# Weight sums on VectorE, a turn inside an early tile, and row sums in two exact parts: one change to an encoder layer

## The chip, the cores and the metric

The kernel runs on one core of a Trainium2 chip. The core has five engines that run side by side: TensorE (PE: matrix products into the accumulators of PSUM; its weight loads, PEld, overlap the products), VectorE (DVE), ScalarE (ACT), GpSimd (POOL) and SyncE (SP, which here only issues transfers from memory). The metric is the device time of one execution in microseconds. Three runs of the kernel before gave 828.65, 829.03 and 829.23, median 829.03.

## The reference

One layer of a bidirectional encoder, 512 positions, width 1024, all in float32:

```
h  = rmsnorm(x, g_pre_mix)
q, k, v, g, u, sv, a_ret, a_sgu = split(h @ w_in)
y_ret = (layernorm(retention(q, k, v)) * silu(g)) @ w_ret_o      # both directions
sv    = layernorm(gelu(sv))                                      # with gain and bias
mixed = einsum('gpq,bnqgc->bnpgc', w_spatial, sv) + b_spatial
y_sgu = (gelu(u) * mixed) @ w_sgu_o
x1 = x  + rmsnorm((sig(a_ret)*y_ret + sig(a_sgu)*y_sgu) @ w_out, g_post_mix)
h2 = rmsnorm(x1, g_pre_ffn)
a, b = split(conv3(h2 @ w_up) + conv_b)
y  = x1 + rmsnorm((gelu(a) * b) @ w_down, g_post_ffn)
```

The mixing multiplies 128 x 128 weights per group with the normed sv. The bias of that norm is the same for all positions, so it enters the mixed result as bias times the row sum of the weights; these row sums are what the kernel calls `rws`.

## The kernel before

**Two parts for each number.** The kernel splits each operand into a high part in the format fp32r (a rounding copy on ScalarE) and a low part, the rest (a subtraction on VectorE): `split`, lines 84 to 86. A product is then three fp32r matmuls (high x high, high x low, low x high), `mm3`, lines 212 to 215. Two products are left in plain float32: the mixing itself (L736) and the row sums of its weights, a matrix of ones times the transposed weights `wst` (L713).

**Seven products for eight.** For u, the two gates and the 16 middle tiles of the up projection (in eight couples), a pair of weight blocks is multiplied in the Winograd way: a 2 x 2 arrangement of weight quarters B11, B12, B21, B22 takes seven products, with the sums of weights T1 = B11 + B12, T3 = B12 + B22, T2 = T1 + B22 and T4 = T2 + B21 (signs are in the stored weights). `w_form`, lines 153 to 171, loads a pair as two transfers of 128 x 1024, makes the sums (T1 and T3 on VectorE, lines 164 and 165; T2 and T4 on GpSimd, lines 166 and 168), and splits each form into a weight slot. `Pair`, lines 647 to 706, makes the products (L663). There are 20 pairs: four of u, eight of the gates, eight of the up projection.

**The order.** `units` lists all weight blocks and forms in the order in which PE needs them; `w_get` prepares them ahead, up to nine slots deep. Each weight form takes one of nine slots (tag `w4`), each raw block one of four raw buffers; a transfer from SP waits until its raw buffer is free. Within these limits the compiler's planner sets the order of each engine's instructions: each engine takes the next instruction in the program's order that by the planner's own times is ready, and on the chip each engine then runs its list strictly in that order, waiting on semaphores. So an instruction can overtake another in the list, but never on the chip.

**Where the change acts.** (1) `w_form`. (2) The row sums: L709 loads `wst`, L713 multiplies, L715 copies the result out. The program places them just ahead of u's pairs and behind the second `g_evac`, which multiplies o by the gate on VectorE (L609), turns it by 16 transposes on PE (L599) and splits it. (3) The start of the up projection. `norms` (lines 842 to 868) ends the mixing for 128 positions and norms them (xn); `turn` (lines 872 to 894) transposes these by eight matmuls (L879), copies the high part with ScalarE (L881), takes the low part with VectorE (L884), and makes a second copy for the Winograd sums (L892). While the last turns are under way, PE works on the first four tiles of the up projection, `early` (lines 898 to 907): first the columns of positions 0 to 255, which need turns 0 and 1, and later those of 256 to 511.

Lines 917 to 923 order that:

```
917    early(0, 0)
918    turn(2, zs[2])
919    for e in range(1, EARLY):
920        early(e, 0)
921    turn(3, zs[3])
922    for e in range(EARLY):
923        early(e, 1)
```

Of the kernel before, what the change touches and what calls it, by code (L numbers as in the profile page):

```python
# [11 lines left out]
F32R = mybir.dt.float32r  # L12
AF = mybir.ActivationFunctionType
ALU = mybir.AluOpType

P = 128
D = 1024
S = 512
NT = S // P
KD = D // P  # L20
# [17 lines left out]
EARLY = 4  # L38
# [9 lines left out]
def tile_block(ctx: ExitStack, tc, xT, x, wall, par, cs, wsp, bsp, gpost, gffn, out):  # L48
    nc = tc.nc
    sb = ctx.enter_context(tc.tile_pool(name="sb", bufs=1))  # L50
# [9 lines left out]
    def blk(dt=F32, n="blk", shape=(P, S)):  # L60
        return sb.tile(list(shape), dt, tag="blk", bufs=NBLK, name=nm(n))

    def tmp(n="tmp", shape=(P, S)):
        return sb.tile(list(shape), F32, tag="tmp", bufs=6, name=nm(n))

    def halves(n):
        return [blk(n=n), blk(n=n)]
# [4 lines left out]
    def ps(shape=(P, S)):  # L72
        return pp.tile(list(shape), F32, tag="ps", name=nm("ps"))

    def const(n, shape):
        return sb.tile(list(shape), F32, tag=n, bufs=1, name=n)
# [4 lines left out]
    def as32(t):  # L81
        return t.bitcast(F32)

    def split(hi, lo, src):
        copy(hi, src)
        nc.vector.tensor_sub(lo, src, as32(hi))  # L86
# [31 lines left out]
    w_ready, w_pos, w_held, w_raw = {}, [0, 0], [0], {}  # L118

    def raw_tile():  # L120
        return sb.tile([P, 1024], F32, tag="raw", bufs=4, name=nm("raw"))

    def slot(n, at=0, w=1024):
        return sb.tile([P, 1088], F32R, tag="w4", bufs=9, name=nm(n))[:, at : at + w]
# [28 lines left out]
    def w_form(form, i):  # L153

        if form == "B11":
            a, b = raw_tile(), raw_tile()
            nc.sync.dma_start(a, wall[i])
            nc.sync.dma_start(b, wall[i + 1])
            w_raw["B11"], w_raw["B12"] = a[:, :S], a[:, S:]
            w_raw["B22"], w_raw["B21"] = b[:, :S], b[:, S:]  # L160
        elif form == "T1":
            t = raw_tile()
            w_raw["T1"], w_raw["T2"], w_raw["T3"], w_raw["T4"] = t[:, :S], t[:, S:], w_raw["B12"], t[:, S:]
            nc.vector.tensor_add(w_raw["T1"], w_raw["B11"], w_raw["B12"])  # L164
            nc.vector.tensor_add(w_raw["T3"], w_raw["B12"], w_raw["B22"])
            nc.gpsimd.tensor_tensor(out=w_raw["T2"], in0=w_raw["T1"], in1=w_raw["B22"], op=ALU.add)  # L166
        elif form == "T4":
            nc.gpsimd.tensor_tensor(out=w_raw["T4"], in0=w_raw["T2"], in1=w_raw["B21"], op=ALU.add)
        w = slot("wf", 16)
        split(w[:, :S], w[:, S:], w_raw[form])  # L170
        return w[:, :S], w[:, S:]
# [21 lines left out]
    def w_unit(u):  # L193
        return w_block(u[1]) if u[0] == "blk" else (w_down if u[0] in "qt" else w_form)(*u)
# [4 lines left out]
    def w_get(look=LOOK):  # L199

        i = w_pos[0]
        w_pos[0] += 1
        room = 2 * look + (2 if w_size(units[i]) == 2 else 0)
        n = sum(w_size(u) for u in units[i : w_pos[1]])
        while w_pos[1] < len(units) and (w_pos[1] <= i or n + w_size(units[w_pos[1]]) <= max(room, 9 if look == LOOK else 0)):
            u = units[w_pos[1]]
            w_ready[w_pos[1]] = w_unit(u)
            w_pos[1] += 1
            n += w_size(u)
        return w_ready.pop(i)  # L210

    def mm3(o, ah, al, bh, bl, start, stop):
        nc.tensor.matmul(o, ah, bh, start=start, stop=False)  # L213
        nc.tensor.matmul(o, ah, bl, start=False, stop=False)  # L214
        nc.tensor.matmul(o, al, bh, start=False, stop=stop)  # L215
# [14 lines left out]
    def col(i):  # L230
        return part[:, i : i + 1]
# [30 lines left out]
    for k in range(KD):  # L262
# [18 lines left out]
        for m in range(8):  # L281
            c = slice(m * P, (m + 1) * P)
# [5 lines left out]
    T0, T1 = slice(0, 256), slice(256, 512)  # L288
# [15 lines left out]

    ident = const("ident", [P, P])
    make_identity(nc, ident)
    ones = const("ones", [P, P])
    nc.gpsimd.memset(ones, 1.0)
    wst = blk(n="wst")
    nhalf = const("nhalf", [P, 16])  # L310
    nc.gpsimd.memset(nhalf, -0.5)
# [10 lines left out]
    for t in range(NT):  # L322
        for n in range(2):
# [3 lines left out]
                out=xt, in_=xt, func=AF.Square, accum_out=ss[:, 4 * n + t : 4 * n + t + 1]  # L327
# [19 lines left out]
    for c in range(19, 1, -2):  # L347
        v.scalar_tensor_tensor(
            out=lc, in0=lc, scalar=1.0 / c, in1=lb, op0=ALU.add, op1=ALU.mult
# [4 lines left out]
        out=lg, in0=lc, scalar=-2.0, in1=lg, op0=ALU.mult, op1=ALU.add  # L354
# [5 lines left out]
    for m in range(8):  # L360
        t = blk(n="qkraw")
# [8 lines left out]
    for t in range(NT):  # L370
# [4 lines left out]
            start=True,  # L375
            stop=True,
# [249 lines left out]
    for n, acc in enumerate(t_group()):  # L626
        if n < 2:
            for k in (n + 2, n + 6):
                t = tmp("xT")
# [80 lines left out]
    bst = blk(n="bst")  # L710
    nc.gpsimd.dma_start(bst, bsp.rearrange("g p -> (g p)")[None, :].to_broadcast([P, S]))
    rw = ps()
    nc.tensor.matmul(rw, ones, wst, start=True, stop=True)  # L713
    rws = blk(n="rws")
    copy(rws, rw)  # L715
    uT, late = [], None
    for j in range(KD // 2):
        p = Pair(AF.Gelu_apprx_tanh, lambda: blk(n="u"), None, rbc)
# [51 lines left out]
    for j in range(KD // 2):  # L770
        for o, t in gated_pair(ogh, ogl, late if j == 0 else None):
            b = blk(n="r")
# [99 lines left out]
    def turn(t, zs):  # L872
        c = slice(t * P, (t + 1) * P)
        pf = []
        for n in range(2):
            p = ps()
            for f in range(4):
                pf.append(p[:, f * P : (f + 1) * P])
                nc.tensor.transpose(pf[-1], zs[n][:, f * P : (f + 1) * P], ident)  # L879
            for k in range(4 * n, 4 * n + 4):  # L880
                nc.scalar.activation(  # L881
                    out=h2h[k][:, c], in_=pf[k], func=AF.Copy, scale=col(FFNG + k)
                )
                v.scalar_tensor_tensor(  # L884
                    out=h2l[k][:, c], in0=pf[k], scalar=col(FFNG + k), in1=as32(h2h[k][:, c]),
                    op0=ALU.mult, op1=ALU.subtract,
                )
        for k in range(KD):
            if t == 0 and k % 2 == 0:
                h2.append(halves("h2"))  # L890
            at = (k % 2) * 256 + (t % 2) * P
            nc.scalar.activation(  # L892
                out=h2[k // 2][t // 2][:, at : at + P], in_=pf[k], func=AF.Copy, scale=col(FFNG + k)
            )

    early_w, early_o = [], []

    def early(e, q):

        if q == 0:  # L900
            early_w.append(w_get(1))
            early_o.append(ps())
        wh, wl = early_w[e]
        f = slice(q * 256, (q + 1) * 256)
        for k in range(KD):
            c = slice(k * P, (k + 1) * P)
            mm3(early_o[e][:, f], wh[:, c], wl[:, c], h2h[k][:, f], h2l[k][:, f], k == 0, k == KD - 1)

# [2 lines left out]
    for t in range(NT):  # L911
# [3 lines left out]
        acc.append(dn_.finish(t, 1))  # L915
        zs[t] = norms(t, acc)
    early(0, 0)
    turn(2, zs[2])
    for e in range(1, EARLY):
        early(e, 0)  # L920
    turn(3, zs[3])
    for e in range(EARLY):
        early(e, 1)

# [70 lines left out]
    while i < NF:  # L995
        if i in couples:
            p = Pair(None, lambda: tmp("c"), (h2h, h2l, h2forms))
# [179 lines left out]
def _parts(a, n, w):  # L1177

    k = a.shape[0] // P
    return a.reshape(k, P, n, w).transpose(2, 1, 0, 3).reshape(n, P, k * w)  # L1180
# [15 lines left out]
def _two(a):  # L1196

    b = _parts(a, 8, P).reshape(4, 2, P, 2, S)
    return np.stack([
        np.concatenate([b[:, 0, :, 0], b[:, 1, :, 0]], -1), np.concatenate([b[:, 1, :, 1], b[:, 0, :, 1]], -1),  # L1200
    ], 1)


def _up(a):

    for i, _ in COUPLES:
        b, c = a[2 * i].reshape(P, 2, S), a[2 * i + 1].reshape(P, 2, S)
        a[2 * i : 2 * i + 2] = np.stack([
            np.concatenate([b[:, 0], c[:, 0]], -1), np.concatenate([c[:, 1], b[:, 1]], -1),
        ])  # L1210
    return a


def _gates(a, w):

    return np.concatenate([_two(a), _parts(w, 8, P).reshape(4, 2, P, 1024)], 1).reshape(16, P, 1024)
# [79 lines left out]
```

## Time and profile before

| | |
|---|---|
| median of 3 runs | 829.03 us |
| profiled execution: its time, and its span from first to last instruction | 830.36 us, 828.6 us |
| PE busy | 818.5 us (99% of the span), 5152 matmuls |
| VectorE busy | 658.0 us (79%), 1100 instructions |
| ScalarE busy | 439.7 us (53%), 769 instructions |
| GpSimd busy | 101.1 us (12%), 102 instructions |
| the two GpSimd sums (L166, L168) | 36.5 and 26.5 us, 20 times each |
| PE's clock as granted | 0.998 |

A row of a timeline has the start in the span, the duration, engine, line, operation, what it writes and reads (by the program's names, buffer numbers left out), and in brackets how long the engine had been idle and what ended that. Several alike in a run stand in one row with their number. Matmuls are pipelined: one of 512 columns is shown as 0.39 us long, but the next starts 0.23 us later, so that it is the distance of the starts that counts. The same holds on VectorE in a smaller measure. A group's row ends with count, busy time and mean length in ns, and then the idle time ahead of its instructions and what ended it.

### The profile page before, as it was taken

The numbers are of one execution on the slowest core, as the hardware profiler recorded it, in microseconds if no ns is written. First come the engines' busy times: TensorE is split into PE (matmuls) and PEld (weight loads), VectorE is DVE, ScalarE is ACT, GpSimd is POOL, SyncE is SP. The second block draws the span as 40 slices with busy tenths as digits, with TensorE's granted clock in tenths as the row PEclk, the third lists the DMA queues.
The fourth block names the chain that finished last, engine by engine and source line by source line (L and its number), as shares of the span: only waits on it lengthen the run. The fifth ranks groups of instructions, "written<-read, shape, count | busy, mean of one in ns | idle before, by whom it ended". The sixth has DMA issues, their size and how long they took to land.

```text
span 828.6 us, 13261 instructions
## 1 busy us (share of the span) xinstructions
PE 818.5 (99%) x5152; PEld 737.4 (89%) x5152; DVE 658.0 (79%) x1100; ACT 439.7 (53%) x769; POOL 101.1 (12%) x102
## 2 busy tenths in 40 slices
PE   9999999999999999999999999999999999999996
PEld 7888888888899999999988898899999998999996
DVE  7479897877798777767766569979899889987967
ACT  6635445546665444444445585555556666555531
POOL 0010000102121111132210211120201200000001
PEclk9999999999999999999999999999999999999999
DMA  8733222212233332233349112333333341233344
GB/s 292 246 115 102 77 77 76 77 51 93 75 101 129 102 102 82 97 101 101 100 160 339 53 45 72 102 103 102 102 102 102 102 153 51 75 115 104 116 153 153
DMA packets 29215, 93.24 MB, mean 113 GB/s; under 512 B 3360, under 2 KB 4000, under 8 KB 29152
## 3 DMA queue, kind: packets, MB, share of 16 engines
q1 hardware_dynamic: 26928, 86.85, 31.6%
q0 software_dynamic: 1360, 4.46, 1.6%
q10 hardware_dynamic: 864, 1.09, 0.4%
q8 instruction: 40, 0.66, 0.3%
q14 instruction: 23, 0.19, 0.1%
HBM read 88.19 MB, written 4.19 MB: 112 GB/s over the span
## 4 chain that ended last, share of the span: by engine, by line
PE 92%; DVE 5%; ACT 1%; issue 1%; DMA 0%; POOL 0%; DVEq 0%; SPq 0%; POOLq 0%; ACTq 0%
PE ps L663 24%; PE ps L213 12%; PE ps L214 12%; PE ps L215 12%; PE ps L1033 8%; PE ps L475 5%; PE ps L474 5%; PE ps L476 5%; PE ps L1049 2%; PE ps L812 2%; PE ps L811 2%; PE ps L813 2%; PE ps L736 1%; DVE fl L86 1%; PE ps L275 1%; DVE dl L86 1%
## 5 line engine op out<-in xcount | busy, mean ns | idle before, releaser
L86 DVE TENSOR_TENSOR wl<-raw,wh 128x1024 fp32r<-128x1024 f32 (+1 forms) x93 | 108.0, 1170 | 53.1 <-PE ps L663 29.1
L79 ACT ACTIVATE wf<-raw 128x512 fp32r<-128x512 f32 x140 | 85.0, 627 | 98.8 <-PE ps L214 41.1
L86 DVE TENSOR_TENSOR wf<-raw,wf 128x512 fp32r<-128x512 f32 x140 | 109.0, 793 | 25.5 <-ACT wf L79 23.7
L663 PE MATMUL ps<-sh,wf 128*128 128x256 f32 x640 | 122.4, 281 | 0.0
L79 ACT ACTIVATE wh<-raw 128x1024 fp32r<-128x1024 f32 (+2 forms) x95 | 93.3, 991 | 38.7 <-DMA raw<-wall 19.1
L663 PEld LDWEIGHTS ps<-sh,wf 128*128 128x128 f32 x640 | 101.7, 188 | 0.8 <-ACT u L79 0.2
L213 PE MATMUL ps<-h2h,wh 128*128 128x512 f32 (+1 forms) x256 | 92.5, 364 | 0.4 <-ACT h2h L881 0.4
L214 PE MATMUL ps<-h2l,wh 128*128 128x512 f32 (+1 forms) x256 | 92.5, 363 | 0.0
L215 PE MATMUL ps<-h2h,wl 128*128 128x512 f32 (+1 forms) x256 | 92.3, 361 | 0.0
L663 PE MATMUL ps<-sl,wf 128*128 128x256 f32 x320 | 89.9, 281 | 0.0
L474 PE MATMUL ps<-wh,xh 128*128 128x512 f32 x192 | 75.0, 391 | 0.0
L475 PE MATMUL ps<-wl,xh 128*128 128x512 f32 x192 | 74.9, 390 | 0.0
L476 PE MATMUL ps<-wh,xl 128*128 128x512 f32 x192 | 74.8, 390 | 0.0
L166 POOL TENSOR_TENSOR raw<-raw,raw 128x512 f32<-128x512 f32 x20 | 36.5, 1825 | 237.5 <-DVE raw L164 209.3
L663 PEld LDWEIGHTS ps<-sl,wf 128*128 128x128 f32 x320 | 61.3, 192 | 0.6
L1033 PE MATMUL ps<-dl,fh 128*128 128x256 f32 x216 | 60.0, 278 | 0.1
L1033 PE MATMUL ps<-dh,fh 128*128 128x256 f32 x216 | 60.0, 278 | 0.0
L1033 PE MATMUL ps<-dh,fl 128*128 128x256 f32 x216 | 59.9, 277 | 0.0
L663 PE MATMUL ps<-xh,wf 128*128 128x256 f32 x288 | 55.3, 282 | 0.0
L215 PEld LDWEIGHTS ps<-h2h,wl 128*128 128x128 f32 x256 | 48.1, 188 | 7.7
L213 PEld LDWEIGHTS ps<-h2h,wh 128*128 128x128 f32 x256 | 47.8, 188 | 7.6 <-ACT h2h L881 0.7
L214 PEld LDWEIGHTS ps<-h2l,wh 128*128 128x128 f32 x256 | 48.1, 188 | 6.6
(307 smaller groups left out, 2048.2 us busy)
## 6 DMA issues: line engine op xcount, KB each, us to landing
raw<-wall SPq DMA_DIRECT2D x145, 512.0 KB, 3.6
x<-x SPq DMA_DIRECT2D x24, 256.0 KB, 5.4
xT<-xT SPq DMA_DIRECT2D x8, 256.0 KB, 5.3
x<-x POOLq DMA_DIRECT2D x8, 256.0 KB, 2.4
xT<-xT POOLq DMA_DIRECT2D x4, 256.0 KB, 3.9
out<-zg SPq DMA_DIRECT2D x4, 256.0 KB, 2.0
out<-zs ACTq DMA_DIRECT2D x3, 256.0 KB, 3.7
cs<-cs SPq DMA_DIRECT2D x2, 256.0 KB, 4.3
```

The costliest lines, as they stand in the source:

```text
L79: nc.scalar.activation(out=o, in_=i, func=AF.Copy)
L86: nc.vector.tensor_sub(lo, src, as32(hi))
L166: nc.gpsimd.tensor_tensor(out=w_raw["T2"], in0=w_raw["T1"], in1=w_raw["B22"], op=ALU.add)
L213: nc.tensor.matmul(o, ah, bh, start=start, stop=False)
L214: nc.tensor.matmul(o, ah, bl, start=False, stop=False)
L215: nc.tensor.matmul(o, al, bh, start=False, stop=stop)
L474: nc.tensor.matmul(acc[t], xh[k][:, c], wh[:, f], start=k == 0, stop=False)
L475: nc.tensor.matmul(acc[t], xh[k][:, c], wl[:, f], start=False, stop=False)
L476: nc.tensor.matmul(acc[t], xl[k][:, c], wh[:, f], start=False, stop=k == KD - 1)
L663: nc.tensor.matmul(o, w_[:, c], a_, start=first and k == n == 0, stop=k == 3 and n == 2, skip_group_check=True,)
L811: nc.tensor.matmul(o, ah, bh, start=k == 0, stop=False)
L1033: nc.tensor.matmul(o, a_[:, c], w_[:, f], start=j == t == i == 0, stop=j == DP - 1 and i == 2 and n not in (M2, M3, M4), skip_group_check= ...
```

## The change

The sums. A pair's quarters are stored in another arrangement: the first transfer brings B11 and B22, the second B12 and B21. T1 and T3 are then one VectorE operation of 128 x 1024 elements that adds B12, read twice, to both halves of the first block. T2 and T4 are made on VectorE too, each in its own step of the list of forms (a new step "T2"), in place of B12 and B21.

The row sums. The ones become an fp32r matrix (filled by GpSimd into a block, copied by ScalarE); `wst` is split into two parts; two fp32r matmuls take the place of the one in float32. A one is exact in any part, and two parts hold the weight.

The turn. The fourth early tile's first half is cut at k = 5 of 8: the last turn stands between its two pieces.

```
@@ w_form
-            w_raw["B11"], w_raw["B12"] = a[:, :S], a[:, S:]
-            w_raw["B22"], w_raw["B21"] = b[:, :S], b[:, S:]
+            w_raw["both"], w_raw["B12"], w_raw["B21"] = a, b[:, :S], b[:, S:]
+            w_raw["B11"], w_raw["B22"] = a[:, :S], a[:, S:]
         elif form == "T1":
             t = raw_tile()
-            w_raw["T1"], w_raw["T2"], w_raw["T3"], w_raw["T4"] = t[:, :S], t[:, S:], w_raw["B12"], t[:, S:]
-            nc.vector.tensor_add(w_raw["T1"], w_raw["B11"], w_raw["B12"])
-            nc.vector.tensor_add(w_raw["T3"], w_raw["B12"], w_raw["B22"])
-            nc.gpsimd.tensor_tensor(out=w_raw["T2"], in0=w_raw["T1"], in1=w_raw["B22"], op=ALU.add)
+            w_raw["T1"], w_raw["T3"], w_raw["T2"], w_raw["T4"] = t[:, :S], t[:, S:], w_raw["B12"], w_raw["B21"]
+            two = "p (n c) -> p n c"
+            nc.vector.tensor_tensor(
+                out=t.rearrange(two, n=2), in0=w_raw["both"].rearrange(two, n=2),
+                in1=w_raw["B12"][:, None, :].to_broadcast([P, 2, S]), op=ALU.add,
+            )
+        elif form == "T2":
+            nc.vector.tensor_add(w_raw["T2"], w_raw["T1"], w_raw["B22"])
         elif form == "T4":
-            nc.gpsimd.tensor_tensor(out=w_raw["T4"], in0=w_raw["T2"], in1=w_raw["B21"], op=ALU.add)
+            nc.vector.tensor_add(w_raw["T4"], w_raw["T2"], w_raw["B21"])
@@ constants
-    ones = const("ones", [P, P])
-    nc.gpsimd.memset(ones, 1.0)
+    ones = sb.tile([P, P], F32R, tag="ones", bufs=1, name="ones")
+    one = blk(n="one", shape=(P, P))
+    nc.gpsimd.memset(one, 1.0)
+    copy(ones, one)
@@ row sums
-    nc.tensor.matmul(rw, ones, wst, start=True, stop=True)
+    wsth, wstl = parts(wst, "wst")
+    nc.tensor.matmul(rw, ones, wsth, start=True, stop=False)
+    nc.tensor.matmul(rw, ones, wstl, start=False, stop=True)
@@ early
-    def early(e, q):
+    def early(e, q, ks=range(KD)):
...
-        if q == 0:
+        if q == ks.start == 0:
...
-        for k in range(KD):
+        for k in ks:
@@ order
-    for e in range(1, EARLY):
+    for e in range(1, EARLY - 1):
         early(e, 0)
+    early(EARLY - 1, 0, range(0, 5))
     turn(3, zs[3])
+    early(EARLY - 1, 0, range(5, KD))
```

Two functions on the host, `_two` and `_up`, store the quarters in the new arrangement.

More of the change, by code (lines that the diff above doesn't have):

```diff
@@ L1199, in _two @@
     return np.stack([
-        np.concatenate([b[:, 0, :, 0], b[:, 1, :, 0]], -1), np.concatenate([b[:, 1, :, 1], b[:, 0, :, 1]], -1),
+        np.concatenate([b[:, 0, :, 0], b[:, 1, :, 1]], -1), np.concatenate([b[:, 1, :, 0], b[:, 0, :, 1]], -1),
     ], 1)
@@ L1208, in _up @@
         a[2 * i : 2 * i + 2] = np.stack([
-            np.concatenate([b[:, 0], c[:, 0]], -1), np.concatenate([c[:, 1], b[:, 1]], -1),
+            np.concatenate([b[:, 0], c[:, 1]], -1), np.concatenate([c[:, 0], b[:, 1]], -1),
         ])
```

## The prediction

> **What bounds the kernel now.** I read the page first: span, engines, slices.
>
> ```profile
> span 828.6 us, 13261 instructions
> PE 818.5 (99%) x5152; PEld 737.4 (89%) x5152; DVE 658.0 (79%) x1100; ACT 439.7 (53%) x769; POOL 101.1 (12%) x102
> DVE  7479897877798777767766569979899889987967
> PEclk9999999999999999999999999999999999999999
> ```
>
> PE is busy for 818.5 of 828.6 us at an undiminished clock; no other engine reaches 80% on average, but DVE has slices of 9. So time can be won in two ways only: less work on PE, or fewer PE gaps. The second view, the waits of PE and of its weight loads, shows how little there is in gaps:
>
> ```profile
> PE ps L213 <- ACT h2h L881: 0.4, 1, 0.4
> PE ps L599 <- DVE o L609: 0.3, 1, 0.3
> PEld ps L663 <- ACT c L79: 0.4, 1, 0.4
> PEld ps L1033 <- DVE dl L86: 0.3, 1, 0.3
> ```
>
> Past the start, PE waits four times, each below 0.6 us: the ceiling of what removed gaps can give is about 2 us, and two of these places are touched by the change. The third view, DVE's busy time in stretches of the up projection and the start of the down projection, shows where a slower DVE would reach PE (columns: length, PE, weight loads, DVE, ACT, POOL):
>
> ```profile
> 601.50:622.50 21.00, 21.00 (x135) 19.06 (x135) 19.79 (x32) 13.01 (x23) 1.64 (x1) 1.00 0.32 101
> 664.20:685.00 20.80, 20.80 (x134) 18.86 (x133) 18.39 (x30) 13.06 (x21) 0.00 (x0) 1.00 0.46 153
> 685.00:711.00 26.00, 26.00 (x126) 21.88 (x125) 25.48 (x44) 15.86 (x25) 0.00 (x0) 1.00 0.18 61
> 711.00:740.00 29.00, 28.90 (x243) 28.57 (x242) 28.86 (x52) 16.44 (x26) 0.59 (x1) 1.00 0.23 74
> ```
>
> In the couples of the up projection DVE keeps as little as 1.2 us free in 21; from 685 to 740 it has no free time, and PE's 0.3 us wait for dl falls there. No weight sum is made after 664 (POOL is at 0.00), so the sums cannot load that stretch directly.
>
> **Part 1, the sums of a pair's weights.**
>
> ```profile
> L166 POOL TENSOR_TENSOR raw<-raw,raw 128x512 f32<-128x512 f32 x20 | 36.5, 1825 | 237.5 <-DVE raw L164 209.3
> L168 POOL TENSOR_TENSOR raw<-raw,raw 128x512 f32<-128x512 f32 x20 | 26.5, 1326 | 75.8 <-DVE wf L86 71.9 <-ACT cv L930 3.9
> L164 DVE TENSOR_TENSOR raw<-raw 128x512 f32<-128x512 f32 x20 | 13.8, 688 | 2.7 <-DMA raw<-wall 2.6
> L165 DVE TENSOR_TENSOR raw<-raw,raw 128x512 f32<-128x512 f32 x20 | 17.1, 855 | 1.2 <-DMA raw<-wall 1.0
> L182 DVE TENSOR_TENSOR raw<-raw 128x512 f32<-128x512 f32 x18 | 12.4, 688 | 6.9 <-DMA raw<-wall 6.8
> L86 DVE TENSOR_TENSOR wl<-raw,wh 128x1024 fp32r<-128x1024 f32 x81 | 100.5, 1242 | 51.5 <-PE ps L663 29.1 <-issue 7.4 <-PE ps L214 5.8
> L86 DVE TENSOR_TENSOR wf<-raw,wf 128x512 fp32r<-128x512 f32 x140 | 109.0, 793 | 25.5 <-ACT wf L79 23.7 <-PE ps L215 0.8
> L86 DVE TENSOR_TENSOR wl<-raw,wh 128x512 fp32r<-128x512 f32 x12 | 7.5, 686 | 1.6 <-ACT wh L79 1.6
> 213.29 1.28 DVE L609 TENSOR_TENSOR o<-o,g 128x512 f32<-128x512 f32 x2
> ```
>
> There are 20 pairs. POOL loses 20 x (1825 + 1326) ns = 63 us of work; it is idle nearly all the time, so that by itself is worth nothing. DVE: two back-to-back 128x512 operations take 1.28 us (last row), so one more costs 1.28 - 0.69 = 0.6 us of DVE. T2 and T4 therefore add 1.2 us a pair. T1 and T3 go from two operations (1.28 us) to one of 1024 elements; L182 shows that a broadcast operand costs no more than L164 (688 both), so I take the 1.24 us of the 128x1024 row: nothing won to speak of. Against this stands what POOL's operations cost DVE while they ran: L165 lasts 855 where L164 lasts 688, and each of the seven splits of a pair 793 where the same split of a resident block lasts 686: 0.17 + 7 x 0.107 = 0.92 us a pair. Net DVE: +1.2 - 0.9 = +0.3 us a pair, 6 us over the kernel; bounds +1.2 (nothing given back) and, since a broadcast could also let the one operation be shorter, about 0. PE does not see either: even +1.2 a couple stands against 1.2 to 2.4 us free in some 21. ACT's copy of T2 now follows DVE by one operation instead of POOL's 1.8 us, and the weight slots stay the same (the buffer of T1 and T3 is free after T3, that of T4 after T4, that of B11 and B22 last, as three buffers before), so SP's queue of loads sees no later release. PE effect of the sums in the steady state: 0, bounds -0.3 (the wait for c, which stands beside such a sum) and +0.5.
>
> How DVE and POOL got in each other's way, in three rows:
>
> ```profile
> 535.64 1.64 POOL L166 TENSOR_TENSOR raw<-raw,raw 128x512 f32<-128x512 f32 x1 [13.05 <-DVE raw L164]
> 536.17 1.66 DVE L86 TENSOR_TENSOR wf<-raw,wf 128x512 fp32r<-128x512 f32 x1
> 513.70 3.42 POOL L166 TENSOR_TENSOR raw<-raw,raw 128x512 f32<-128x512 f32 x1 [27.25 <-DVE raw L164]
> ```
>
> In the first two DVE's split lasts 1.66 instead of 0.69; in the third it was POOL that lasted 3.42, amid an unbroken run of DVE work that wasn't slowed. The Trainium skill's page "SBUF — State Buffer", section "Who interferes with whom", says that a DVE instruction with two SBUF inputs and a GpSimd instruction that reads SBUF exclude each other for a whole instruction, whichever issues first. Taken for all 40 sums at full length, that rule would give DVE back up to some 60 us (an estimate from the two POOL rows) and make DVE lighter by over 30; the measured means give back only 18. I go by the means.
>
> **Part 2, the row sums of the mixing, and the gate's transposes before them.**
>
> ```profile
> 208.50 1.16 ACT L79 ACTIVATE wf<-raw 128x512 fp32r<-128x512 f32 x2 [4.29 <-PE ps L475]
> 209.16 1.29 DVE L86 TENSOR_TENSOR wf<-raw,wf 128x512 fp32r<-128x512 f32 x2 [4.14 <-ACT wf L79]
> 211.58 1.78 DVE L165 TENSOR_TENSOR raw<-raw,raw 128x512 f32<-128x512 f32 x1
> 215.15 0.69 DVE L609 TENSOR_TENSOR o<-o,g 128x512 f32<-128x512 f32 x1
> 213.91 0.44 PE L599 MATMUL ps<-ident,o 128*128 128x128 f32 x2
> 214.62 1.31 PE L599 MATMUL ps<-ident,o 128*128 128x128 f32 x10 [0.27 <-DVE o L609]
> 215.77 1.02 PE L713 MATMUL ps<-wst,ones 128*128 128x512 f32 x2
> 216.63 0.60 PE L599 MATMUL ps<-ident,o 128*128 128x128 f32 x4
> 204.61 0.39 PE L475 MATMUL ps<-wl,xh 128*128 128x512 f32 x1
> 204.84 0.39 PE L476 MATMUL ps<-wh,xl 128*128 128x512 f32 x1
> ```
>
> The f32 matmul L713 stands as two records and holds PE from 215.77 to 216.63: 0.86 us. An fp32r matmul of 512 columns holds it for 0.23 (204.61 to 204.84); two take 0.46. Saved: 0.40 us, directly on the path. Added: the split of wst, one ACT copy (about 0.6) and one DVE subtraction (0.69). wst is loaded long before, and ACT has stood idle for 4.29 and DVE for 4.14 us up to 209, which covers both; without that cover the matmuls would wait up to 1.3 us. The copy of ones (128x128, about 0.4 of ACT) and POOL's memset lie in the first 50 us, where PE's matmuls are limited by neither; price 0, at most 0.4.
>
> The wait beside it: DVE's L165 lasts 1.78 us under POOL's sum and puts back the gate's products L609, for which the transposes wait (213.91, two of them, then nothing until 214.62: about 0.5 us lost). After the change the double sum lasts 1.24 and T2 may slip in for 0.6. The last product cannot end before 215.84 (it starts when its ACT input is there), so the last four transposes cannot start before 215.9 rather than at 216.63: at most 0.7 us from parts 1 and 2 together. I take -0.6; bounds -0.9 (the products earlier too) and +0.3 (T2 and the split of wst ahead of the last product).
>
> **Part 3, the last turn inside the fourth early tile.**
>
> ```profile
> 486.48 0.89 DVE L864 TENSOR_SCALAR xn<-x,qr 128x512 f32<-128x512 f32 x2 [0.80 <-POOL qr L830]
> 488.43 1.04 PE L879 MATMUL ps<-ident,xn 128*128 128x128 f32 x8
> 489.90 0.74 PE L213 MATMUL ps<-h2h,wh 128*128 128x256 f32 x4 [0.43 <-ACT h2h L881]
> 487.66 0.37 ACT L881 ACTIVATE h2h<-ps,part 128x128 fp32r<-128x128 f32 x1 [0.88 <-DVE h2l L884]
> 488.44 1.14 ACT L892 ACTIVATE h<-ps,part 128x128 f32<-128x128 f32 x4 [0.42 <-DVE h2l L884]
> 489.46 0.64 ACT L881 ACTIVATE h2h<-ps,part 128x128 fp32r<-128x128 f32 x2
> ```
>
> The eight transposes start at 488.43, take eight steps of 0.11, and PE then has nothing until 489.90: about 0.6 us lost. Nine matmuls of 256 columns (k = 5 to 7, three each; 0.12 apart, as four last 0.74 with a tail) move behind the transposes: 1.06 us of cover. The transposes then start at 487.37. The normed rows xn are ready at 486.48 + 0.89 = 487.37, the first half earlier, so they just meet; no wait, or 0.1. But the first copy of the turn, ACT's L881 at 489.46, is not late because of the transposes: ACT was still at the four L892 of the turn before. If ACT's order stays, the copy comes at 489.46 all the same and nothing is won: 0. ACT stood idle for 0.42 us ahead of those L892, long enough for a 0.37 us copy; if the planner, which orders each engine's queue by what is ready, puts it there, the whole 0.6 us goes. I take -0.4, nearer to that idle row, bounds -0.6 and +0.1. Next late is DVE's h2l for the same tiles, which follows each copy.
>
> **The sum.** -0.6 - 0.4 and -0.1 for the wait for c: -1.1 us. The profiled execution has a span of 828.6 and a time of 830.36, 1.3 above the median of the runs, 829.03; the difference lies outside the span, so I take the sum off the median: **827.9 us**.
>
> **Rivals.** What can be told from no change here is about 0.2%, 1.7 us: below 827.4 is faster, above 830.7 slower.
>
> *Nothing but the row sums is won.* ACT's order holds the turn, and T2 fills what L165 leaves: -0.4 to 0: 828.8. For it: the ACT rows above. Chance 0.27.
>
> *More is won.* All four gaps go (0.6 + 0.5 + 0.3 + 0.4) with the 0.4 of L713, as DVE, freed of POOL, is earlier everywhere: -2.0: 827.0. For it: splits at 1.66. Against: DVE gains 0.9 and pays 1.2. Chance 0.23.
>
> *Slower: DVE reaches the stretch from 685 late.* That stretch passes any DVE lateness to PE one for one (25.48 of 26.00, 28.86 of 29.00). The planner arranges every queue anew; should the last two pairs' sums, 2 x (1.24 + 1.2) = 4.9 us, pile up on DVE behind other work, they meet 20.80 - 18.39 = 2.4 us of free time in the couple from 664 and PE waits 2.5: 831.5. It decides once DVE is over 2.4 us late at 664. Against it: a pair's net addition is 0.3. Chance 0.13.
>
> The forecast (827.4 to 828.6) has the remaining 0.37. The range takes in the bounds of the terms, from -2.3 to +1.0, with a tenth left out on either side: 826.7 to 830.1. Faster by over 0.2%: 0.25 (the second rival and an edge of the forecast); within: 0.62; slower: 0.13.
>
> **What would show it.** The POOL groups of L166 and L168 gone and a 128x1024 DVE sum of about 1.24 us; splits wf back near 690 ns; the row sums as two records 0.23 apart, and the last transposes at about 216; PE's wait for h2h below 0.2. The prediction is wrong if PE shows a new wait for wf (T2 or T4 late on DVE), if dl's wait at 739 grows, or if the normed rows come after the moved transposes.

## The result, and the profile after

The changed kernel takes 834.04 us (median of four runs, 833.31 to 835.36), the kernel before 828.9 beside it (828.65 to 829.23): 1.0058 times the time, interval 1.0043 to 1.0074. It is slower by 5.1 us, where the prediction had 827.9 and a range up to 830.1. The profiled execution has a span of 832.1 us and a time of 833.84.

The page of the changed kernel first (engine, busy us and share, instructions):

```profile
span 832.1 us, 13187 instructions
PE 819.1 (98%) x5152; PEld 737.6 (89%) x5152; DVE 662.9 (80%) x1121; ACT 440.8 (53%) x771; POOL 38.1 (5%) x62
```

PE does the same number of matmuls in nearly the same busy time; POOL has lost 63 us, DVE gained 4.9. The loss is not to be seen here. It is in the waits of PE (what PE waited for: us in total, times, the longest):

```profile
PE ps L720 <- ACT wst L79: 2.3, 1, 2.3
...
PE ps L605 <- DVE o L615: 0.6, 2, 0.4
PE ps L217 <- ACT h2h L889: 0.4, 1, 0.4
```

One long wait is new, and it is longer than all four of before in the same view together (2.2 us): the row sums (L720, before L713) wait 2.3 us for ACT's copy of `wst`, which the change has added. The wait for h2h, which the moved turn was to shorten, stands at 0.4 as before. The timeline of both engines at the new wait (start, duration, instruction, idle time before it and what ended that):

```profile
208.95 1.16 ACT L79 ACTIVATE wf<-raw 128x512 fp32r<-128x512 f32 x2 [4.23 <-PE ps L481]
...
215.49 0.62 ACT L79 ACTIVATE wf<-raw 128x512 fp32r<-128x512 f32 x1
216.76 2.06 ACT L79 ACTIVATE gh<-ps 128x512 fp32r<-128x512 f32 x4 [0.65 <-PE ps L605]
218.69 0.65 ACT L79 ACTIVATE wst<-wst 128x512 fp32r<-128x512 f32 x1
216.40 0.66 PE L605 MATMUL ps<-ident,o 128*128 128x128 f32 x4 [0.36 <-DVE o L615]
219.40 0.63 PE L720 MATMUL ps<-wst,ones 128*128 128x512 f32 x1 [2.34 <-ACT wst L79]
219.83 0.41 PE L669 MATMUL ps<-xh,wf 128*128 128x256 f32 x1
220.04 0.42 PE L669 MATMUL ps<-xl,wf 128*128 128x256 f32 x1
```

ACT was idle for 4.23 us up to 208.95 with `wst` long in place, and did not copy it there. The copy stands behind the four copies gh, which wait for the last gate transposes; PE's list has the row sums right behind those transposes, so PE stops for the length of all five copies. The last two rows show something more: 256-column matmuls start 0.21 us apart, where before they started 0.12 apart. The stretches around the wait (length; PE, weight loads, DVE, ACT and POOL busy; granted clock; DMA):

```profile
217.00:219.30 2.30, 0.05 (x1) 0.00 (x0) 2.30 (x4) 2.30 (x5) 0.00 (x0) 1.00 0.00 0
219.30:220.50 1.20, 1.10 (x5) 1.01 (x6) 1.20 (x3) 0.04 (x1) 0.00 (x0) 0.63 0.00 0
220.50:223.00 2.50, 2.50 (x12) 2.40 (x12) 0.16 (x1) 0.60 (x1) 0.00 (x0) 0.50 0.02 7
223.00:230.00 7.00, 6.98 (x61) 6.78 (x60) 3.67 (x7) 3.73 (x8) 0.00 (x0) 1.00 0.20 74
```

After the idle stretch the clock is granted at 0.5 (12 matmuls in 2.5 us; afterwards 61 in 7.0). From the 0.63 and the 0.50 follow 0.9 + 2.5 = 3.4 us at half speed, which cost PE half of that, 1.7 us.

Where the 5.1 us lie is read from the starts of named matmuls. The stages: A from the first gate transpose of the second `g_evac` to the first matmul of the mixing; B to the last high x high matmul of the product with w_out; C to the first couple of the up projection (the turns and the early tiles); D to the first matmul of the down projection; E the first 150 matmuls of that, and F the rest up to the start of PE's last matmul.

| us | A | B | C | D | E | F |
|---|---|---|---|---|---|---|
| before, profiled | 63.86 | 197.78 | 47.29 | 188.76 | 17.67 | 91.30 |
| after, profiled | 66.20 | 197.76 | 48.23 | 188.59 | 17.67 | 91.08 |

A and C are longer, D is shorter by the wait for c, the rest stands to 0.2 us. The profiled execution of before was itself 1.6 us longer in A: the same code takes 62.25 in another execution (run e3_turn; the last section shows the difference). Against that, A has lost 3.95, C 0.94, D has won 0.17, and 0.5 lie ahead of A, where executions of the same code differ by as much: 5.2 in all, against 5.1 measured.

### The profile page after: what moved, and what is told of

It is laid out like the page before. It is cut to its first block, busy times and chain, and to the rows that moved or that the text cites. A ratio compares the mean times of both kernels' runs of the same rounds, so it can differ in the third digit from the quotient of the medians.

```text
span 832.1 us, 13187 instructions
## 1 busy us (share of the span) xinstructions
PE 819.1 (98%) x5152; PEld 737.6 (89%) x5152; DVE 662.9 (80%) x1121; ACT 440.8 (53%) x771; POOL 38.1 (5%) x62
## 5 line engine op out<-in xcount | busy, mean ns | idle before, releaser
L86 DVE TENSOR_TENSOR wl<-raw,wh 128x1024 fp32r<-128x1024 f32 (+1 forms) x93 | 106.2, 1150 | 56.0 <-PE ps L669 34.9
L86 DVE TENSOR_TENSOR wf<-raw,wf 128x512 fp32r<-128x512 f32 x140 | 97.8, 714 | 24.1 <-ACT wf L79 23.8
L217 PE MATMUL ps<-h2h,wh 128*128 128x512 f32 (+1 forms) x256 | 93.1, 365 | 0.4 <-ACT h2h L889 0.4
L218 PE MATMUL ps<-h2l,wh 128*128 128x512 f32 (+1 forms) x256 | 92.9, 364 | 0.0
L219 PE MATMUL ps<-h2h,wl 128*128 128x512 f32 (+1 forms) x256 | 92.2, 361 | 0.0
L217 PEld LDWEIGHTS ps<-h2h,wh 128*128 128x128 f32 x256 | 47.9, 188 | 7.7 <-ACT h2h L889 0.6
L219 PEld LDWEIGHTS ps<-h2h,wl 128*128 128x128 f32 x256 | 47.9, 188 | 7.7
L218 PEld LDWEIGHTS ps<-h2l,wh 128*128 128x128 f32 x256 | 48.2, 189 | 7.0 <-DVE h2l L892 0.4
L79 ACT ACTIVATE dh<-raw 128x768 fp32r<-128x768 f32 (+1 forms) x36 | 33.7, 949 | 30.1 <-DVE raw L191 15.4
```

Of the source, the lines that this page charges most:

```text
L79: nc.scalar.activation(out=o, in_=i, func=AF.Copy)
```

## The experiments

The theories after this result: the wait for `wst` and the halved clock behind it cost most of the time (F in the expectations: it is the idle time that halves the clock); the turn costs about one; the sums cost nothing. The rival for the sums is that of the prediction, DVE late in the up projection. For the place of the copy there were two: its buffers, and its place in the program (A2).

**Each part alone.** e1_sums is the kernel before with the new `w_form` and storage only:

```
+            nc.vector.tensor_tensor(out=t.rearrange(two, n=2), in0=w_raw["both"].rearrange(two, n=2),
+                in1=w_raw["B12"][:, None, :].to_broadcast([P, 2, S]), op=ALU.add)
+        elif form == "T2":
+            nc.vector.tensor_add(w_raw["T2"], w_raw["T1"], w_raw["B22"])
```

> The kernel before with part 1 alone (T1 and T3 in one VectorE operation, T2 and T4 on VectorE). Theory A (the loss is the row sums' wait with the halved clock behind it, and a smaller one at the turn): PE keeps its matmul rate and its four waits below 0.6 us; time within 0.5 us of the kernel before. Rival B (the sums make VectorE late): +2 us or more, with a wait of PE for wf, sh or dl that the kernel before does not have.

Measured: 830.77 us, 1.0001 times before (0.9986 to 1.0016). No wait for a split weight appeared; D is 188.59, with the wait for c gone. The rival "DVE late" falls: B, C, D and E are equal to before's to 0.2 us or better.

e2_rows has the row sums in two parts only:

```
+    wsth, wstl = parts(wst, "wst")
+    nc.tensor.matmul(rw, ones, wsth, start=True, stop=False)
+    nc.tensor.matmul(rw, ones, wstl, start=False, stop=True)
```

> The kernel before with part 2 alone (row sums in two fp32r parts). Theory A: the copy of wst stands behind the four copies gh on ScalarE, PE waits about 2.3 us for it at 217, its clock is halved for about 3 us behind that, and the time is 2.5 to 4 us above the kernel before. Rival B (the sums are to blame): no more than 0.5 us either way. Rival C (wait and saving cancel, 2.3 against 0.4, without the clock): +1.9.

Measured: 833.88, 1.0050 (1.0030 to 1.0069). Its waits of PE and its timeline of ACT:

```profile
PE ps L716 <- ACT wst L79: 2.3, 1, 2.3
```

```profile
216.69 2.06 ACT L79 ACTIVATE gh<-ps 128x512 fp32r<-128x512 f32 x4 [0.65 <-PE ps L601]
218.61 0.65 ACT L79 ACTIVATE wst<-wst 128x512 fp32r<-128x512 f32 x1
```

This part by itself makes the wait, at the same place, and nearly the whole loss.

e3_turn has the cut early tile only:

```
+    early(EARLY - 1, 0, range(0, 5))
     turn(3, zs[3])
+    early(EARLY - 1, 0, range(5, KD))
```

> The kernel before with part 3 alone (the last turn at k = 5 of the fourth early tile). Theory A: ScalarE's first copy of the turn comes no earlier, as it waits behind the copies of the turn before; PE's gap stays at 0.6 us, and the matmuls behind it, now in another order, wait several times more for h2h and h2l: +0.5 to +1.0 us. Rival D (what was predicted): the gap closes, -0.4 us.

Measured: 830.01, 1.0004 (0.9987 to 1.0020). The time alone says nothing, but C is 48.22 against 47.29, as in the full change (48.23). So the turn's part of the loss is its own, 0.93 us.

**The place of the copy.** `parts` takes its two tiles from the pool of 76 general blocks. e4_rows_tmp is e2_rows with two buffers of another tag, its line in the program unchanged:

```
-    wsth, wstl = parts(wst, "wst")
+    wsth, wstl = (sb.tile([P, S], F32R, tag="tmp", bufs=6, name=nm("wst")) for _ in range(2))
+    split(wsth, wstl, wst)
```

> Part 2 alone, the two parts of wst taken from the six buffers of tag tmp instead of the 76 of tag blk; nothing else differs from the second kernel of this call. Theory A1 (the copy stood late because all 76 buffers were taken until the gate's products were turned): ScalarE makes the copy before 216 and PE does not wait for it; time 0 to 0.8 us below the kernel before. Rival A2 (it stands late because it comes late in the program): the copy stays behind gh, PE waits about 2.3 us, time as in the second kernel.

Measured: 832.06, 1.0013 (0.9998 to 1.0027). PE has no wait for `wst`; ACT's timeline:

```profile
215.08 0.62 ACT L79 ACTIVATE wst<-wst 128x512 fp32r<-128x512 f32 x1
```

The copy comes 3.5 us earlier, ahead of gh, though nothing but the buffer has changed: it was the buffers, and A2 falls. The likely reason is that all 76 blocks are taken until the gate products o, which are blocks too, have been turned; the views leave buffer numbers out, so this is argued and not shown. From the other buffers the copy still does not stand in ACT's long idle time, which had ended 6 us earlier. Its profiled execution was longer in F (94.25), which this edit does not touch.

e5_after_tmp is the full change with the same edit.

> The changed kernel, with the two parts of wst in buffers of tag tmp, nothing else. Theory A1 (slots): the copy of wst stands ahead of gh, PE has no wait for it and no halved clock, and the sh products of the first pair of u begin 4 us earlier than in the changed kernel; what is left is the turn: 0 to +1.0 us against the kernel before. Rival E (the changed kernel is slow for other reasons too): still over +2 us.

Measured: 829.54, 1.0009 (0.9998 to 1.0020). The wait is gone and A is 62.05 instead of 66.20:

```profile
215.28 0.62 ACT L79 ACTIVATE wst<-wst 128x512 fp32r<-128x512 f32 x1
```

```profile
215.96 0.50 PE L721 MATMUL ps<-wst,ones 128*128 128x512 f32 x1
216.30 0.60 PE L605 MATMUL ps<-ident,o 128*128 128x128 f32 x4
216.65 0.36 PE L669 MATMUL ps<-xh,wf 128*128 128x256 f32 x1
216.86 0.44 PE L722 MATMUL ps<-wst,ones 128*128 128x512 f32 x1
217.13 0.28 PE L669 MATMUL ps<-xl,wf 128*128 128x256 f32 x1
```

The upper row is ACT, the lower are PE: the row sums find their operands, and u begins at 216.65 instead of 219.83.

e7_sums_rows_tmp leaves the turn where it was (parts 1 and 2, the same buffers).

> The kernel before with part 1 and part 2, the two parts of wst in buffers of tag tmp; no turn. Theory A: the saving of the f32 matmul and of the gate's wait, 0.3 to 1.0 us below the kernel before. Rival B: VectorE is late somewhere, +1 us or more.

Measured: 828.72, 0.9994 (0.9982 to 1.0007), where e5_after_tmp had 829.54. C is 47.57, 0.6 less than with the turn.

**Idle time and clock.** e6_after_fill is the full change with work for PE put ahead of the row sums; the copy keeps its bad place:

```
+    for _ in range(12):
+        nc.tensor.matmul(rw, ones, xh[0], start=True, stop=True)
     nc.tensor.matmul(rw, ones, wsth, start=True, stop=False)
```

> The changed kernel, with twelve fp32r matmuls more of 512 columns, whose result is overwritten, ahead of the row sums: 2.7 us of PE work that fills the wait for the copy of wst, which stays behind gh. Theory F (the idle 2.3 us halves PE's clock, and that costs 1.5 to 2 us more): the clock stays at 1.00 behind it, the fillers cost about what the wait cost, and the time is 1 to 2 us below the changed kernel, some 2.5 to 4 above the kernel before. Rival G (the halved clock has another cause): the clock falls here too, time as the changed kernel or 0.4 above.

Measured: 833.99, 1.0044 (1.0029 to 1.0060), with the profiled execution at 831.43. ACT's copy still came at 218.18. PE's timeline and the same stretches as above:

```profile
216.30 2.55 PE L721 MATMUL ps<-xh,ones 128*128 128x512 f32 x10
```

```profile
219.30:220.50 1.20, 1.20 (x12) 1.16 (x11) 0.85 (x2) 0.00 (x0) 0.00 (x0) 1.00 0.05 14
220.50:223.00 2.50, 2.50 (x23) 2.46 (x23) 1.47 (x4) 2.03 (x4) 0.00 (x0) 1.00 0.00 0
```

The clock stays at 1.00. Ten of the twelve matmuls stand in the place of the wait, the other two in the gap ahead of the last four transposes. From the start of the last transpose to the kernel's own next matmul it is 2.41 us here (216.27 to 218.68) and 2.61 in the change (216.78 to 219.40). A is 64.33 instead of 66.20: 1.87 less, of which 0.2 is that difference. The halved clock was thus worth about 1.7 us, the half of its 3.4. The median does not show it (833.99 against 834.04): three of the seven runs take 831.43 to 831.74 and four 833.99 to 834.67, and the reading rests on the clock and the stage.

In e2_rows the clock fell later. PE was at work again from 219.32 on, and its clock went down only at 221.0, again for 3.4 us:

```profile
219.30:221.00 1.70, 1.64 (x9) 1.34 (x10) 1.10 (x2) 0.01 (x1) 0.00 (x0) 1.00 0.00 0
221.00:224.40 3.40, 3.40 (x18) 3.40 (x17) 0.69 (x1) 1.49 (x3) 0.00 (x0) 0.50 0.02 5
```

So the moment at which the clock falls is not given by the wait alone.

**The turn.** ACT's first copies keep their pace from before to after; what differs is the place of the transposes and the order of PE's list. Of before (the prediction shows the transposes at 488.43 and the first copies h2h at 489.46):

```profile
490.26 0.62 ACT L881 ACTIVATE h2h<-ps,part 128x128 fp32r<-128x128 f32 x2 [0.16 <-DVE h2l L884]
490.47 0.28 PE L214 MATMUL ps<-h2l,wh 128*128 128x256 f32 x1
490.59 0.28 PE L215 MATMUL ps<-h2h,wl 128*128 128x256 f32 x1
```

Of after:

```profile
491.31 1.14 ACT L900 ACTIVATE h<-ps,part 128x128 f32<-128x128 f32 x4 [0.42 <-DVE h2l L892]
492.32 0.64 ACT L889 ACTIVATE h2h<-ps,part 128x128 fp32r<-128x128 f32 x2
493.13 0.62 ACT L889 ACTIVATE h2h<-ps,part 128x128 fp32r<-128x128 f32 x2 [0.16 <-DVE h2l L892]
490.23 1.03 PE L887 MATMUL ps<-ident,xn 128*128 128x128 f32 x8
492.76 0.38 PE L217 MATMUL ps<-h2h,wh 128*128 128x256 f32 x1 [0.44 <-ACT h2h L889]
493.15 0.38 PE L218 MATMUL ps<-h2l,wh 128*128 128x256 f32 x1
493.55 0.38 PE L217 MATMUL ps<-h2h,wh 128*128 128x256 f32 x1
493.93 0.38 PE L218 MATMUL ps<-h2l,wh 128*128 128x256 f32 x1
```

From the start of stage C (475.55 before, 478.37 after) the transposes come at 11.86 instead of 12.88, 1.02 earlier. The first copy comes at 13.95 instead of 13.91: it still stands behind the four second copies (L900, before L892) of the turn before. So PE has the same 0.4 us wait. Then the lists part. Before, PE has four L213 in one row, which read as the first slice of four tiles, and was never held up for more than 0.04 us again. After, L217, L218 and L219 take turns, which reads as one tile slice by slice, and the slices wait for their copies: starts at 492.76, 493.15, 493.55, 493.93. The 16 matmuls from 492.76 to 495.73 take 2.97 us where 16 x 0.117 = 1.87 would do: 1.1 lost, against 0.94 in the stage.

e8_turn_defer tried to free the copy by writing the second copies later in the program:

```
     turn(3, zs[3])
+    second(2, pf2)
```

> The kernel before with part 3 alone, and the second copies (h2) of the last two turns put behind the fourth early tile in the program, so that ScalarE has the last turn's first copies next. Theory A (ScalarE's order holds the first copy back): the first copy of the last turn comes at least 1 us earlier against its transposes, PE's gap falls from 0.9 to below 0.3 us and the time is 0.5 to 1 us below part 3 alone. Rival H (the copies and VectorE's low parts, one after the other, are what PE waits for, whoever stands ahead): gap and waits stay, time as part 3 alone.

Measured: 830.78, 1.0021 (1.0006 to 1.0036). The list of ACT stayed as it was, the four second copies at 488.25 and the first ones at 489.26: the edit did not do what it was for and settles nothing.

e9_turn_force is e3_turn with that order tied: the second copies of the third turn are issued after the last turn's first copies.

```
+    with tc.issue_after(firsts[3].ins):
+        second(2, pf2)
+    second(3, pf3)
```

> Part 3 alone, with the second copies (h2) of the last two turns tied on ScalarE behind the eight first copies of the last turn, so that those really stand next in its list (the attempt before this left them where they were). Theory A (ScalarE's order holds the first copy back): the first copy of the last turn comes about 1 us earlier against its transposes, PE's gap of 0.6 to 0.9 us falls below 0.2, and the stage from the end of the mixing's output to the first couple falls from 48.2 us to 47.3 or less. Rival H (the chain of copies and low parts is what PE waits for): the stage stays at 48.0 or above.

Measured: 829.47, 0.9992 (0.9983 to 1.0001). PE's wait is gone and C is 46.87 (e3_turn: 48.22; before: 47.29). On ACT:

```profile
485.86 3.52 ACT L883 ACTIVATE h2h<-ps,part 128x128 fp32r<-128x128 f32 x9 [1.91 <-DVE h2l L886]
489.28 4.24 ACT L900 ACTIVATE h<-ps,part 128x128 f32<-128x128 f32 x16
```

All first copies stand in a row now, and the second ones behind them.

e10_before_force has the tie without the cut.

> The kernel before with that tie alone, the turn where it was (behind the whole fourth tile). Theory A: the transposes end at the same time as in the kernel before and the first copy follows them at once instead of 0.2 to 0.5 us later: the stage falls from 47.29 us by 0.1 to 0.5 us. If the cut at k = 5 does what was meant once the order is right, the kernel ahead of this one in the call is 0.3 to 0.9 us below this one; if the tie does all of it, they agree within 0.2.

Measured: 830.48, 1.0012 (1.0003 to 1.0022). C is 47.21, 0.08 less than before, and e9's 46.87 is 0.34 less again. D grew by 1.07, to 189.83. A new wait of PE holds it, in the first couple of the up projection:

```profile
PE ps L663 <- ACT c L79: 0.9, 1, 0.9
```

Three splits wf stand right ahead of this copy on ACT (524.60, 1.66 us in all), where e9 has one. e11 and e12 have the tie too, with D at 188.59.

**Together.** e11_after_tmp_force is the full change with both edits.

> The changed kernel with both faults mended: the two parts of wst in buffers of tag tmp, and the tie on ScalarE. Theory A: nothing of the loss is left, the f32 matmul's and the gate's saving of 0.2 to 0.5 us and the turn's come through: 0.5 to 1.5 us below the kernel before. Rival E: something else in the change costs time, at or above the kernel before.

Measured: 827.66, 0.9983 (0.9970 to 0.9996). e12_sums_rows_force is the same with the last turn in its old place.

> As the kernel ahead of this one in the call, with the last turn where it was in the kernel before (behind the whole fourth tile). Theory A: between the kernel before and the one ahead; the difference to that one is what the cut at k = 5 gives by itself, 0.3 to 0.9 us. If the cut is worth nothing, the two agree within 0.2 us in the stage from the end of the mixing's output to the first couple.

Measured: 827.96, 0.9981 (0.9973 to 0.9990). Both beat the kernel before and the change. A is 61.86 in both; C is 46.74 with the cut and 46.89 without, a difference of 0.15, too little to tell in the times.

These two differences in C, 0.34 and 0.15, can't be put down to the cut. C holds 192 distances from one 256-column matmul to the next, and most are either about 113 or about 118 ns (the last section has more on that). The close ones were 72 before, 16 in e10, 78 in e9, 73 in e12 and 140 in e11. With each of them put at 118, C would be 47.60 before, 47.28 in e10, 47.22 in e9, 47.20 in e12 and 47.36 in e11 (an estimate from the starts in these traces). The tie is then worth 0.2 to 0.4 us with the cut or without it, and a gain by the cut is not shown.

## Why the prediction was wrong

**The sums: right.** The double sum was put at 1.24 us, DVE's net at +6 us with bounds, the effect on PE at 0. DVE's groups after (count | busy, mean ns | idle before):

```profile
L165 DVE TENSOR_TENSOR raw<-raw,raw 128x1024 f32<-128x1024 f32 x20 | 24.4, 1218 | 1.8 <-DMA raw<-wall 1.8
L172 DVE TENSOR_TENSOR raw<-raw 128x512 f32<-128x512 f32 x20 | 13.7, 687 | 0.3
L170 DVE TENSOR_TENSOR raw<-raw,raw 128x512 f32<-128x512 f32 x20 | 13.7, 683 | 0.2
L86 DVE TENSOR_TENSOR wf<-raw,wf 128x512 fp32r<-128x512 f32 x140 | 97.8, 714 | 24.1 <-ACT wf L79 23.8
```

1218 ns; the splits fell from 793 to 714; DVE's total rose by 4.9; e1_sums shows no time. The means were the better guide: the estimate that counted all 40 sums at full length would have made DVE lighter by over 30 us, and it became heavier. A sum's full length is not what it takes from DVE: of the 3.42 us in the prediction's third row, all but 1.15 passed before DVE's own L165 ended (515.28 to 515.97), so POOL may well have waited for DVE there.

**The row sums: here the prediction failed, at the sentence that ACT's idle 4.29 us and DVE's 4.14 "covers both".** The idle time was there, and after the change still is (4.23), but the copy did not go there: it came at 218.69, behind the copies gh. I had looked at when the input is ready and when the engine is free, and not at where the output goes. e4 and e5 show that the output's buffers put it behind gh. They do not show that free buffers bring it into the idle time: in e5 that ended at 208.74 and the copy came at 215.28, early enough for PE all the same. Why no run used the idle time stays open. The sentence on the cover gone priced the wait at "up to 1.3 us", one copy and one subtraction: it took the split to begin when PE asked. It stood behind four other copies: 2.34. And no term at all stood for what comes after an idle PE. Of A's 66.20 - 61.86 (e11_after_tmp_force) = 4.34 us, 2.5 is the gap itself (2.61 between the starts, less the 0.11 of a transpose), 1.7 the halved clock and 0.1 the rest. With its copy in time, the part wins 0.4 together with the sums (61.86 against e3_turn's 62.25 and e9's 62.21), where I had 0.6.

On that second term the trace comes first: idle for 2.34 us, then 0.5 for 3.4 us; filled, 1.00 throughout. The Trainium skill's page "TensorE: Matmul & The Clock Gate", section "What's actually happening", has TensorE's clock at half after an idle window of about 3.4 us, and back at full after a busy one. The half agrees, and 3.4 us is how long it lasted; the idle time here was shorter. The same page of the Trainium skill, section "HAM oscillation — how this bites in real kernels", allows gaps up to about 3.4 us; here 2.34, with transposes ahead of it, was enough. The Trainium skill's same page, section "Part 4: PE-mode transpose", says that transposes are not counted as busy in the same way; counted so, the stretch without ordinary matmuls goes from 214.42 to 219.40, 5.0 us, and the two would fit. No run here tells whether that is so.

**The turn: the step that failed is the choice of -0.4.** The prediction named the right question, whether ACT's list stays, and its own value for that case, 0. It took the other because ACT had 0.42 us free ahead of the second copies. The list stayed, and the loss of 0.94 lies beyond its bound of +0.1, as PE's list came out in another order, in which slice after slice waited for a copy. That e9 wins where e3 loses shows that the copies' place was the cause. It does not save the term: by the estimate above, e10 and e12 win about as much by the order of the copies alone, so that no run shows the 0.4 for the cut itself.

**The wait for c: right** (-0.1; D won 0.17).

**The rivals.** "Slower: DVE reaches 685 late" had the right sign by the wrong mechanism: D and E did not move. What the forecast summed to -1.1 is what the profiles of e11_after_tmp_force show once both copies are in time: -0.39 in A, -0.55 in C, -0.17 in D. That the two sums agree is in part luck: A had been put at -0.6, and the gain in C is, by the estimate above, that of the tie, which is no part of the change.

Of the three signs by which the prediction was to be wrong none came: no wait for wf, dl's wait still at 0.3, and no gap ahead of the moved transposes. The wait that came was not on its list. Two of its sums do not come out either. The bounds of its terms add up to -1.8 and +0.9, or +1.3 with the copy of the ones, and not to -2.3 and +1.0; the gains of its second rival make 2.2 and not 2.0. The measured time lies above the range by either count.

## What to carry to other kernels

Where an added instruction is costed at nothing because its engine is idle, check that its output has a free buffer at that time: here the choice of the pool alone put a copy 3.5 us later, behind four others that PE did not need so soon. Even the other pool did not bring it into the idle time. Price a wait of the bounding engine by everything that stands ahead of the awaited instruction, and add what the clock does afterwards. A step moved ahead wins nothing while the engine that takes it over comes no earlier; here the order on that engine was worth 0.2 to 0.4 us, and the move itself nothing that a run shows.

## What had not been expected of the hardware

**A wait of 2.3 us cost about 4.2 us**, by the clock (above); at the turn, with waits of 0.4 us and a loss of 1.1 in all, the matmuls behind them started 0.11 to 0.12 us apart as ever.

**Two spacings at one clock.** Chains of 256-column matmuls run through whole stretches at one of two spacings, in executions whose code in that stage is the same, both at a granted clock of 1.00. Before, in the stage of u, and a stretch of the down projection in e4_rows_tmp (columns as above):

```profile
240.00:260.00 20.00, 20.00 (x172) 20.00 (x172) 18.10 (x30) 12.62 (x24) 4.37 (x3) 1.00 0.35 110
```

```profile
790.00:820.00 30.00, 30.00 (x257) 30.00 (x256) 19.35 (x33) 9.29 (x16) 1.11 (x2) 1.00 0.33 114
```

And e3_turn and before in the same two stretches:

```profile
240.00:260.00 20.00, 20.00 (x179) 20.00 (x178) 18.23 (x30) 12.61 (x24) 4.37 (x3) 1.00 0.34 115
```

```profile
790.00:820.00 30.00, 30.00 (x268) 30.00 (x267) 21.52 (x39) 9.11 (x18) 1.11 (x2) 1.00 0.42 135
```

172 matmuls or 179 in 20 us, 257 or 268 in 30: about 4% apart, 117 and 112 ns. It moves A by about 1.6 us and F by 3.1 (91.1 or 94.2), and so the time of a run by 0.2 to 0.6%, more than any part of this change won. The times of one kernel fall into groups that far apart as well: of e1_sums' twelve runs three took 828.2 to 828.6 and nine 830.7 to 831.4. What sets it is open: it changed with no edit near it, and no run here was made for it. Where intervals above are wide, this is the likely reason.
